# State-space decay: segment sums as two fp32r matmuls instead of one fp32 matmul

## The chip, the cores and the metric

The kernel runs on one core of a Trainium2 chip. The metric is the device time of one execution in microseconds, as the median of several runs of the same program. A program page and a trace of one profiled execution go with it; all rows below come from these.

## What is computed

The reference is a trunk of two layers on a sequence of 1024 tokens of width 1024. In each layer a normed input is projected, the columns go to four groups of heads (two kinds of attention, a state-space group and a gated delta group), their outputs are joined and projected back, and a feed-forward part with a convolution follows. The change lies in the state-space group, which runs once forward and once backward over the sequence in 8 chunks of 128 tokens, with 4 heads. The core of it, cut:

```
acum = cumsum(dt * A within a chunk)
seg = acum[..., :, None] - acum[..., None, :]        # segment sums
decay = exp(where(causal, seg, -inf))
scores = einsum('bcihn,bcjhn->bchij', Cc, Bc) * decay
y_diag = einsum('bchij,bcjhp->bcihp', scores, xc)
```

The rest of the scan (states at the chunk ends, their carry from chunk to chunk, `y_off`) is not touched.

## The kernel before

All tensors are fp32. A product that needs fp32 accuracy is mostly written as several matmuls over fp32r operands: the helper `splits` (L130) writes the high part of a tensor with ScalarE (L133, a copy into fp32r) and the low part with VectorE or GpSimd (L135, source minus high part). Some smaller products, the segment sums among them, are matmuls on plain fp32 operands.

A layer has a mixing part and a feed-forward part. In the mixing part `mix` (L1359) weaves nine streams of work by a table of start and end times, `when` (L439 on): `T` (transposed projections, L254 to L263), `nats` (other projections, `nat_step`, matmul L523, evacuated at L557 to L563), `d_prep` and `d_inverse` (set-up of the delta group, L848 to L931), `mixer_c` (the state-space group), `prep_a`, `att` (all attention: scores L1068, row maximum on VectorE L1070, exponential on ScalarE L1076, transposes L493 with their splits L133 and L135, product L1101), `mixer_d` and `prep_b`. The table gives the order in which the program is traced; after that a list scheduler with its own timing model orders the instructions of each engine, with the priorities that the tracing gave, and buffers are handed out from pools in that order. Each engine then runs its own list strictly in order (TensorE loads weights ahead), and waits on semaphores. So any change of a cost or of a pool's size can reorder the whole mixing part.

SBUF scratch comes from three pools by size, `slots = 34, 12, 24` (L55): 34 tiles of 4 KB per partition (`s4`), 12 of 2 KB (`s2`) and 24 of 1 KB (`s1`). The `s2` pool holds, among others, the split weights `wh` and `wl` of `load_T`, the buffers of `prep_a`, the query tiles of the attention, and the decay tiles `R`.

The state-space group has two halves. The first (L752 on) carries the states over the chunks. The second, the decay stage, goes chunk by chunk in three functions: `early(c + 1)` loads the next chunk and has GpSimd (POOL) write, per direction `d`, the tile `R` of 128 x 512: mask times gate (L780), then `X` (L737) and the skip term `xs` (L784). `decay(c)` makes the scores (matmul L792, masked by VectorE into `sm`, L796), the segment sums as one fp32 matmul of `R` with a triangular mask (L800, one per direction, 512 columns), their exponential on ScalarE back into `R` (L801), the product with `sm` on VectorE (L803), and the part from the carried state (matmul L806, VectorE L809, POOL L811 and L812 into `y`). `finish(c)` multiplies the decayed scores with `X` (L820), adds on VectorE (L821, L822), norms with POOL's power (L143, L144) and stores. Eight chunks in two directions give 16 matmuls of L800 per layer, 32 in the program.

The gates themselves (`ag`, 128 x 8 x 16) are made once per layer in `gates` (L689), from which `ex` and others are derived.

## Time and profile before

| what | value |
|---|---|
| median of 3 runs | 3188.63 us (3188.3 to 3191.51) |
| the profiled execution: span from first to last instruction | 3194.5 us |
| PE, weight loads, DVE, ACT, POOL busy | 95%, 80%, 61%, 39%, 25% |
| decay stage, layer 0 | 400.2 to 485.0 us |
| decay stage, layer 1 | 1987.6 to 2072.4 us |

No time of its own is recorded for the profiled execution beside its span; the span is 5.9 us above the median of the runs. To read it: busy shares are means over stages with different limits, so the rows by stage say more than the totals. PE's busy time counts a matmul to its modelled end, which overlaps with the next one; the time that a stream of matmuls really takes is the distance from start to start. The program places each layer's mixing part ahead of its feed-forward part: in layer 0 the mixing lasts to some 760 us, in layer 1 from 1600 to 2347 us.

### The profile page before, as it was taken

How to read it: one execution, taken by the hardware profiler on the slowest of the kernel's cores; microseconds unless marked ns; L12 is line 12 of the kernel's file. 1: busy time of each engine (PE TensorE's matmuls, PEld its weight loads, DVE VectorE, ACT ScalarE, POOL GpSimd, SP SyncE). 2: the span in 40 equal slices, each digit the busy share in tenths (PEclk: the TensorE clock that was granted, in tenths of full speed). 3: DMA queues.
4: the chain of work that ended last, by engine and by line, in shares of the span. 5: the costliest groups of instructions: out<-in, count | busy, mean ns of one | idle time of the engine just before them, and what ended most of it. 6: DMA issues, size and time to landing. Idle time of an engine off the chain costs nothing. (4 is left out here: it accounts for less than half of the span.)

```text
span 3194.5 us, 48801 instructions
## 1 busy us (share of the span) xinstructions
PE 3043.8 (95%) x18198; PEld 2550.7 (80%) x18198; DVE 1938.1 (61%) x3624; ACT 1251.9 (39%) x2615; POOL 789.4 (25%) x1253
## 2 busy tenths in 40 slices
PE   6998998999999999999999889999999999999997
PEld 6778777887888888888787777788878888888886
DVE  4556687686545555555565475876855455555556
ACT  3333355675432222222243333567743422222221
POOL 1266766221200000000143575753211000000003
PEclk9999999999999999999999998999999999999999
DMA  4255523232321111112232555232323112111212
GB/s 138 64 148 152 142 77 83 69 105 88 112 73 40 47 60 53 40 40 63 75 125 76 148 129 141 81 86 74 100 85 122 53 47 60 53 40 40 61 39 112
DMA packets 384561, 266.76 MB, mean 84 GB/s; under 512 B 147745, under 2 KB 353221, under 8 KB 384325
## 3 DMA queue, kind: packets, MB, share of 16 engines
q1 hardware_dynamic: 384324, 263.64, 28.5%
q8 instruction: 144, 2.36, 0.3%
q14 instruction: 93, 0.75, 0.1%
HBM read 194.54 MB, written 68.94 MB: 82 GB/s over the span
## 5 line engine op out<-in xcount | busy, mean ns | idle before, releaser
L263 PE MATMUL p<-hT,wh 128*128 128x512 f32 x3456 | 960.1, 392 | 7.1 <-ACT cy L388 2.6
L263 PEld LDWEIGHTS p<-hT,wh 128*128 128x128 f32 x3456 | 649.6, 189 | 144.8 <-ACT cy L388 3.4
L263 PE MATMUL p<-hT,wl 128*128 128x512 f32 x1728 | 553.2, 391 | 0.0
L263 PEld LDWEIGHTS p<-hT,wl 128*128 128x128 f32 x1728 | 325.2, 188 | 68.4 <-DVE wl L135 0.9
L221 POOL TENSOR_TENSOR acc<-acc,gain 128x768 f32<-128x768 f32 x14 | 28.9, 2066 | 1413.8 <-ACT junk L177 1413.8
L388 ACT ACTIVATE cy<-p,cw 128x1024 f32<-128x1024 f32 x88 | 106.0, 1204 | 589.7 <-PE p L263 589.7
L389 DVE SCALAR_TENSOR_TENSOR cy<-p,cw,cy 128x1023 f32<-128x1023 f32 x88 | 112.8, 1282 | 358.9 <-ACT cy L388 358.6
L523 PE MATMUL p<-wn,hT 128*128 128x256 f32 (+1 forms) x1920 | 291.1, 306 | 40.5 <-DVE pb L563 17.9
L523 PEld LDWEIGHTS p<-wn,hT 128*128 128x128 f32 x1920 | 266.6, 198 | 51.0 <-DVE pb L563 19.5
L135 DVE TENSOR_TENSOR pT<-pt,pT 128x512 fp32r<-128x512 f32 x256 | 172.6, 682 | 58.4 <-ACT pT L133 57.9
L133 ACT ACTIVATE wh<-raw 128x512 fp32r<-128x512 f32 x216 | 128.0, 624 | 187.1 <-PE p L263 93.3
L133 ACT ACTIVATE pT<-pt 128x512 fp32r<-128x512 f32 x256 | 150.6, 597 | 105.1 <-PE pt L493 95.1
L1070 DVE TENSOR_REDUCE nm<-p 128x1 f32<-128x1024 f32 x128 | 155.0, 1216 | 21.8 <-PE p L1068 21.6
L362 DVE TENSOR_TENSOR acc<-acc,p 128x512 f32<-128x512 f32 x160 | 109.3, 685 | 94.3 <-PE p L358 94.2
L362 DVE TENSOR_TENSOR acc<-acc,pt 128x512 f32<-128x512 f32 x160 | 109.5, 684 | 91.3 <-PE pt L358 89.3
L493 PE MATMUL pt<-ident,p 128*128 128x128 f32 x1024 | 154.5, 278 | 8.3 <-ACT p L1076 4.0
L1403 PE MATMUL p<-wo,oh 128*128 128x512 f32 x512 | 161.7, 394 | 0.3 <-ACT oh L133 0.3
L135 DVE TENSOR_TENSOR wl<-raw,wh 128x512 fp32r<-128x512 f32 x180 | 116.8, 685 | 64.7 <-ACT wh L133 64.7
L1076 ACT ACTIVATE p<-p,nm 128x1024 f32<-128x1024 f32 x128 | 142.3, 1112 | 15.0 <-DVE nm L1070 14.9
L493 PEld LDWEIGHTS pt<-ident,p 128*128 128x128 f32 x1024 | 117.4, 142 | 31.5 <-DVE pT L135 6.7
L358 PE MATMUL p<-owh,gh 128*128 128x512 f32 x352 | 138.6, 394 | 2.4 <-DVE acc L362 2.4
L358 PE MATMUL pt<-owh,gh 128*128 128x512 f32 x352 | 137.7, 391 | 2.9 <-DVE acc L362 2.8
(316 smaller groups left out, 5724.9 us busy)
## 6 DMA issues: line engine op xcount, KB each, us to landing
raw<-in_f_w_in_dram SPq DMA_DIRECT2D x176, 256.0 KB, 3.3
raw<-in_f_w_out_dram SPq DMA_DIRECT2D x88, 256.0 KB, 2.8
raw<-in_w_in_dram SPq DMA_DIRECT2D x72, 256.0 KB, 2.9
raw<-in_w_out_dram SPq DMA_DIRECT2D x32, 256.0 KB, 3.3
xr<-x_mid SPq DMA_DIRECT2D x16, 512.0 KB, 6.6
x_mid<-xr SPq DMA_DIRECT2D x14, 512.0 KB, 2.9
orow<-o_d SPq DMA_DIRECT2D x48, 128.0 KB, 3.0
pa<-pa_d SPq DMA_DIRECT2D x32, 176.0 KB, 3.6
```

Of the source, the lines that this page charges most:

```text
L133: nc.scalar.activation(out=hi, in_=src, func=AF.Copy)
L135: (eng or nc.vector).tensor_tensor(lo, src, hi.bitcast(F32), op=ALU.subtract)
L263: nc.tensor.matmul(pm[:, h * 512:(h + 1) * 512], s[:, k % 4, :], self.h_mov(p, k, h), start=a, stop=b)
L358: nc.tensor.matmul(po, s[i // 2][:, tk], w[:, cs], start=a, stop=b)
L362: nc.vector.tensor_tensor(acc[i][:, cs], acc[i][:, cs], po, op=ALU.add)
L388: nc.scalar.activation(out=y, in_=p, func=AF.Identity, scale=w1, bias=b)
L389: nc.vector.scalar_tensor_tensor(y[:, 1:], p[:, :n - 1], w0, y[:, 1:], op0=ALU.mult, op1=ALU.add)
L493: self.nc.tensor.transpose(pt[:n, t, :], src(4 * c + t), self.ident)
L523: self.nc.tensor.matmul(po, self.h_sta(a, k, i), wt[k][b], start=(k == 0 and a == 0 and b == 0), stop=(k == 7 and a == 1))
L1070: v.reduce_max(nm, s, axis=AX.X, negate=True)
L1076: nc.scalar.activation(out=p, in_=s, func=AF.Exp, bias=nm, accum_out=rs)
L1403: nc.tensor.matmul(y[:, cs], s[k // 2][:, k % 2, :], W[k][w][:, cs], start=(k == 0 and s is oh and w == 0), stop=(k == 7 and s is ol))
```

## The change

The gates of the state-space group are split once per layer into an fp32r high part and the fp32r remainder (`agc`, one ScalarE copy and one VectorE subtraction in `gates`). In `early`, POOL writes two tiles per direction, mask times high part and mask times low part (`Rp`, fp32r, 128 x 512 each), where it wrote one `R`. In `decay`, two fp32r matmuls accumulate into the same PSUM tile with the mask in fp32r (`maskR`, one ScalarE copy at the program's start). The exponential goes to a tile of the old `R` ring, no longer onto its own input. The two new rings take four more `s2` tiles, so that pool grows from 12 to 16; to make room the build reserves less SBUF for a DMA scratch that the SP queue's transfers go without. Three comment lines become empty.

```
-    slots = 34, 12, 24
+    slots = 34, 16, 24
...
+        self.maskR = self.t(self.cst, [128, 2, 128], F32R, "maskR")
+        nc.scalar.activation(out=self.maskR.rearrange("p d c -> p (d c)"), in_=m[:, 256:512], func=AF.Copy)
...
+        self.agc = self.par([128, 2, 8, 8], "agc")
+        nc.scalar.activation(out=self.agc[:, 0].bitcast(F32R), in_=ag[:, :, 0:8], func=AF.Copy)
+        v.tensor_tensor(self.agc[:, 1].bitcast(F32R), ag[:, :, 0:8], self.agc[:, 0], op=ALU.subtract)
...
+        rRh, rRl = (ring(lambda: self.s2([128, 4, 128], F32R, "Rp"), n) for n in (2, 2))
...
-                R = rR()
-                g.tensor_tensor(R, bc(self.mask[d], 1, 4), bc(self.ag[:, c, 4 * d:4 * d + 4], 2, 128), op=ALU.mult)
+                R = []
+                for k, r in ((0, rRh), (1, rRl)):
+                    R.append(r())
+                    g.tensor_tensor(R[k], bc(self.mask[d], 1, 4), bc(self.agc[:, k, c, 4 * d:4 * d + 4], 2, 128), op=ALU.mult)
...
-                nc.tensor.matmul(pseg, self.mask[2 + d], Rs[d], start=True, stop=True)
+                for k in range(2):
+                    nc.tensor.matmul(pseg, self.maskR[:, d], Rs[d][k], start=(k == 0), stop=(k == 1))
+                Rs[d] = rR()
                 nc.scalar.activation(out=Rs[d], in_=pseg, func=AF.Exp)
...
-    nc = _bacc.Bacc("TRN2", target_bir_lowering=False, num_devices=1)
+    nc = _bacc.Bacc("TRN2", target_bir_lowering=False, num_devices=1, dynamic_dma_scratch_size=1024)
```

The built order changes in both layers' mixing parts; in the feed-forward parts the transfers keep their order and some matmuls move by a few places. Line numbers of the changed kernel lie some 2 to 10 above those of the kernel before (its segment matmul is L809, its `Rp` L788).

On POOL in the decay stage of layer 0, one chunk, before: `R` per direction, with `X` (L737) between, then skip term, norm and the sum `y`.

```order
L780 TENSOR_TENSOR R_4051<-masks_292,ag_695 128x512
L737 TENSOR_TENSOR X_3368<-xs_3358,dt_693 128x256
L780 TENSOR_TENSOR R_4053<-masks_292,ag_695 128x512
L737 TENSOR_TENSOR X_3376<-xs_3358,dt_693 128x256
L143 TENSOR_SCALAR rs_588_4237<-ss_4234 128x1
L784 TENSOR_TENSOR xs_3358<-xs_3358,dsk_273 128x256
L144 TENSOR_TENSOR rs_588_4237<-rs_588_4237,mhalf_71 128x1
L811 TENSOR_TENSOR y_4045<-R_4042 128x256
L812 TENSOR_TENSOR y_4045<-y_4045,xs_3354 128x256
```

The same place after, on POOL:

```order
L145 TENSOR_SCALAR rs_594_4256<-ss_4253 128x1
L788 TENSOR_TENSOR Rp_3990<-masks_292,agc_699 128x512
L788 TENSOR_TENSOR Rp_3992<-masks_292,agc_699 128x512
L146 TENSOR_TENSOR rs_594_4256<-rs_594_4256,mhalf_71 128x1
L788 TENSOR_TENSOR Rp_3994<-masks_292,agc_699 128x512
L788 TENSOR_TENSOR Rp_3996<-masks_292,agc_699 128x512
L821 TENSOR_TENSOR y_4058<-R_4055 128x256
L822 TENSOR_TENSOR y_4058<-y_4058,xs_3359 128x256
L743 TENSOR_TENSOR X_3581<-xs_3367,dt_695 128x256
```

Four mask products stand ahead of the sum `y` (L811 before, L821 after) instead of two, the two `X` go behind it, and two of the products stand between the two halves of the norm (L143 and L144 before, L145 and L146 after).

On PE in the same stage, a later chunk, before: scores (L792), segment matmuls (L800), with a transpose of the attention (L493) between, and the matmul on the carried state (L806).

```order
L1320 MATMUL pt_4363<-ident_66,qn_3958 96x128 x4
L493 MATMUL pt_4379<-ident_66,p_4019 128x128 x4
L792 MATMUL p_589_4243<-cz_3364,bt_3360 128x256
L800 MATMUL p_590_4247<-R_3985,masks_292 128x512
L493 MATMUL pt_4386<-ident_66,p_4019 128x128 x4
L800 MATMUL p_591_4251<-R_3987,masks_292 128x512
L806 MATMUL p_592_4255<-Sin_3348,cz_3364 128x256 x2
```

After, on PE:

```order
L1330 MATMUL pt_4390<-ident_66,qn_3963 96x128 x4
L800 MATMUL p_595_4262<-cz_3369,bt_3365 128x256
L495 MATMUL pt_4406<-ident_66,p_4028 128x128 x4
L809 MATMUL p_596_4266<-Rp_3990,maskR_294 128x512
L809 MATMUL p_596_4266<-Rp_3992,maskR_294 128x512
L809 MATMUL p_597_4271<-Rp_3994,maskR_294 128x512
L809 MATMUL p_597_4271<-Rp_3996,maskR_294 128x512
L495 MATMUL pt_4413<-ident_66,p_4028 128x128 x4
L816 MATMUL p_598_4276<-Sin_3353,cz_3369 128x256 x2
```

Four matmuls in a row (two per direction) take the place of two with a transpose between; the scores (L792 before, L800 after) move one transpose forward.

On POOL ahead of the decay stage, some 136 us into layer 0, before: the scaled queries `th` (L629) of both directions, on which transposes on PE wait, and then the mask products of `d_prep` (L852).

```order
L135 TENSOR_TENSOR wl_1460<-raw_1457,wh_1459 128x512
L629 TENSOR_TENSOR th_985<-nat_988,ex_706 128x1024 x2
L852 TENSOR_TENSOR R_1535<-masks_292,ag_695 128x256 x2
L852 TENSOR_TENSOR R_1582<-masks_292,ag_695 128x256 x2
L135 TENSOR_TENSOR wl_1883<-raw_1880,wh_1882 128x512
```

After, on POOL:

```order
L137 TENSOR_TENSOR wl_1465<-raw_1462,wh_1464 128x512
L862 TENSOR_TENSOR R_1540<-masks_292,ag_697 128x256 x2
L862 TENSOR_TENSOR R_1587<-masks_292,ag_697 128x256 x2
L137 TENSOR_TENSOR wl_1888<-raw_1885,wh_1887 128x512
L631 TENSOR_TENSOR th_990<-nat_993,ex_711 128x1024
L866 TENSOR_TENSOR R_1540<-R_1540,masks_292 128x256 x2
L867 TENSOR_TENSOR R_1540<-R_1540,bt_670 128x256
L631 TENSOR_TENSOR th_990<-nat_993,ex_711 128x1024
```

`d_prep` has moved ahead of the queries, and three of its steps (L866 twice, L867) stand between the two directions' `th`.

## Rows read from the trace of the kernel before

**Rows 1.** page: span, busy time per engine, and the span in 40 slices

```profile
span 3194.5 us, 48801 instructions
PE 3043.8 (95%) x18198; PEld 2550.7 (80%) x18198; DVE 1938.1 (61%) x3624; ACT 1251.9 (39%) x2615; POOL 789.4 (25%) x1253
...
PE   6998998999999999999999889999999999999997
...
POOL 1266766221200000000143575753211000000003
PEclk9999999999999999999999998999999999999999
```

**Rows 2.** windows by stage: window, length, busy us (instructions) per engine, TensorE clock, DMA

```profile
0.00:400.00 400.00, 347.07 (x2399) 298.05 (x2400) 223.88 (x526) 147.59 (x311) 194.96 (x291) 0.94 0.47 128
400.20:485.00 84.80, 80.42 (x479) 63.31 (x479) 72.98 (x141) 46.77 (x107) 58.68 (x98) 0.98 0.29 79
485.00:760.00 275.00, 260.21 (x2468) 224.55 (x2467) 211.32 (x491) 188.43 (x424) 91.70 (x177) 0.99 0.31 84
760.00:1600.00 840.00, 828.05 (x3728) 684.15 (x3727) 449.09 (x658) 246.18 (x482) 36.28 (x56) 1.00 0.21 63
...
1987.60:2072.40 84.80, 80.44 (x478) 63.19 (x478) 72.99 (x141) 46.77 (x107) 58.67 (x98) 0.98 0.29 79
```

**Rows 3.** instructions of line 800, who waited: min/median/max ns

```profile
L800 PE MATMUL p<-R,masks x64: 590/593/1193, 400.5 to 2071.7; 128*128 128x512 f32 x64
...
  DVE sm L796: 3.9, 2
...
  ACT R L801: 19.6, 20
```

**Rows 4.** timeline, first chunk of the decay stage: start, us, engine, line

```profile
400.47 1.02 PE L800 MATMUL p<-R,masks 128*128 128x512 f32 x2
...
401.53 0.60 ACT L801 ACTIVATE R<-p 128x512 f32<-128x512 f32 x1 [0.94 <-PE p L800]
```

**Rows 5.** window in the feed-forward stage, fp32r matmuls of 512 columns only

```profile
1000.00:1200.00 200.00, 200.00 (x884) 165.62 (x883) 109.91 (x155) 51.25 (x89) 0.00 (x0) 1.00 0.16 48
```

**Rows 6.** groups by line in 400 to 485 us: busy, mean ns, idle before

```profile
L780 POOL TENSOR_TENSOR R<-masks,ag 128x512 f32<-128x512 f32 x13 | 14.0, 1074 | 4.2 <-PE p L820 3.2 <-ACT p L1076 1.1
L803 DVE TENSOR_TENSOR R<-R,sm 128x512 f32<-128x512 f32 x14 | 10.8, 774 | 0.4 <-ACT R L801 0.4
L811 POOL TENSOR_TENSOR y<-R 128x256 f32<-128x256 f32 x7 | 5.5, 785 | 19.2 <-DVE R L809 19.2
```

**Rows 7.** groups by line in 0 to 400 us: POOL writing fp32r tiles of 512

```profile
L135 POOL TENSOR_TENSOR wl<-raw,wh 128x512 fp32r<-128x512 f32 x18 | 23.9, 1335 | 39.6 <-ACT wh L133 38.0 <-DMA pa_d<-pa 1.5
```

**Rows 8.** waits in 400 to 485 us: total us, times, longest; DVE, then POOL

```profile
DVE rs L1077 <- ACT p L1076: 3.3, 3, 2.2
DVE y L821 <- PE p L820: 1.7, 2, 1.3
...
POOL y L811 <- DVE R L809: 19.2, 5, 6.5
POOL R L780 <- PE p L820: 3.2, 4, 1.2
```

**Rows 9.** two DVE lines with two SBUF inputs: min/median/max ns

```profile
L803 DVE TENSOR_TENSOR R<-R,sm x32: 667/688/1104, 402.2 to 2073.6; 128x512 f32<-128x512 f32 x32
L822 DVE TENSOR_TENSOR y<-y,zc x7: 411/681/1236, 410.1 to 483.2; 128x256 f32<-128x256 f32 x7
```

**Rows 10.** waits of PE in 0 to 400 us

```profile
PE p L523 <- DVE pb L563: 8.8, 4, 3.4
PE pt L493 <- POOL th L629: 4.8, 3, 2.1
```

**Rows 11.** groups by line in 0 to 400 us

```profile
L857 POOL TENSOR_TENSOR R<-R,bt 128x256 f32<-128x256 f32 x16 | 11.6, 740 | 0.0
L856 POOL TENSOR_TENSOR R<-R,masks 128x256 f32<-128x256 f32 x16 | 11.4, 734 | 9.4 <-ACT R L854 9.4
L629 POOL TENSOR_TENSOR th<-nat,ex 128x1024 f32<-128x1024 f32 x4 | 7.6, 1912 | 4.8 <-DVE nat L616 2.7 <-PE pt L493 2.0
```

## The prediction

> **What bounds the kernel now.** I read the page first. PE is busy for 95% of the span and in every slice but the first at least at eight tenths, at full clock nearly throughout; no other engine passes 61% [rows 1]. So a microsecond taken off PE's stream is worth up to a microsecond, if nothing else steps in where it is taken. Then the stages. The segment sums lie in the decay stage, 84.8 us in each layer, and the two layers give the same row but for hundredths [rows 2]. There PE is busy 80.4 us, but DVE has 73.0 (86%) and POOL 58.7 (69%), against 61% and 25% over the span: the change gives PE time back in a stretch in which two other engines are far fuller than elsewhere, and puts the work on one of them. After the stage PE has attention to do until 760 us with DVE at 211 of 275 us and POOL at a third, and then the feed-forward part, where only PE counts. Time won in the decay stage therefore stays won, unless it is lost before the attention takes over.
>
> **What the change takes off PE.** Each of the 32 fp32 matmuls of line 800 stands in the trace as two records of 593 ns [rows 3]. Two of them span 1.02 us, so the second starts 1.02 - 0.593 = 0.427 us after the first [rows 4]: that is the time that each record keeps the stream. An fp32r matmul of the same 512 columns takes 200 us / 884 = 0.226 us from start to start, with its weight load of 128 columns hidden, in a stretch where PE does nothing else [rows 5]. The change puts two fp32r matmuls where two records were, so 64 x (0.427 - 0.226) = 12.9 us leave PE, 6.4 us in each decay stage. The number of weight loads is the same. The chain to the exponential gets shorter too: ScalarE waits 19.6 us in 20 waits on these matmuls [rows 3], and from the start of the first record to the result it will be 0.226 + 0.39 where it was 1.02, some 0.4 us less. That helps those who wait and is not added to the sum.
>
> **What it adds on POOL.** 32 more mask products. One takes 1.07 us, and 13 of a layer's 16 lie in the stage [rows 6], the others just ahead of it. So POOL's 58.7 us become 58.7 + 14.0 = 72.7 us in a stage that should shrink to 84.8 - 6.4 = 78.4 us: 93%. The cover is there: POOL stands 19.2 us in this stage at line 811, waiting for VectorE's line 809, and 3.2 us for line 820 at the old `R` buffers [rows 8]. The order puts the four products of the next chunk right in front of that wait (the POOL rows of the section on the change), so they fill idle time, and the new rings are freed by the segment matmul itself and not by line 820. If that cover were gone, the 14.0 us would be paid in each layer. No row shows POOL writing fp32r from a mask and a broadcast; its fp32r subtraction of 512 columns, with two full inputs, takes 1.34 us [rows 7]. By that end the stage's 26 products cost 34.7 us where 13 now cost 14.0, and POOL needs 79.4 us, a little more than the shortened stage has. I take the 1.07 us, since shape and inputs are the same and only the type of the output differs, and keep the other for the range.
>
> **What it does to VectorE.** Nothing is added in the stage, but VectorE has only 84.8 - 73.0 = 11.8 us left there. It would have 78.4 - 73.0 = 5.4 us left if PE got its whole gain. And it gets slower where POOL works beside it. Line 803, which reads two SBUF tiles, takes 688 ns in the median and up to 1104; line 822 between 411 and 1236 [rows 9]; the mean of line 803 in the stage is 774 [rows 6]. With POOL at 93% instead of 69% I add 0.09 us (774 - 688, the delay that it has now, once more) on each of some 14 calls, and as much over the other lines of this kind together: 2 us or a bit more per stage, as an estimate; at the worst each of 14 calls waits 1104 - 688 = 0.42 us, 5.8 us. VectorE then needs 75 us of 78.4. Its waits come from chains that pass through PE and ScalarE (lines 1077, 821) [rows 8], of which some always remain. So I don't take the whole 6.4 us but two thirds, 4.2 us per layer: the stage then lasts 80.6 us with VectorE at 93%.
>
> The trace shows line 822 stretched to three times its shortest time while POOL runs [rows 9]. The Trainium skill (SBUF — State Buffer, Who interferes with whom) says that a VectorE instruction with two SBUF inputs and a GpSimd instruction that reads SBUF hold each other off for a whole instruction, by who starts first. That speaks against this change: by the mean of the rows the price is the 2 us above, by this rule at its hardest the one that the second rival works out below.
>
> **The rest.** `maskR` is one ScalarE copy of 256 columns before the first projections end; `agc` is one small copy and one small subtraction per layer, at 90 us, where PE has the projections to do. Both at nothing; without that cover under 1 us in all. The smaller DMA scratch: I count nothing, since every transfer that the page of the kernel before lists in this program's issues comes from SP's queue.
>
> **The order in front of the stage.** Four more 2 KB tiles let weights be split and loaded earlier, and the scheduler has reordered the first 400 us of each layer. PE idles 400 - 347 = 53 us there in layer 0 [rows 2], so something can be won or lost. Won: at the second pair of query tiles sixteen small matmuls now cover a wait. Lost: at the first pair (POOL's last rows in the section on the change) two calls of line 856 and one of 857, some 0.74 us each [rows 11], now stand ahead of the second `th`, so that a wait which takes part in the 4.8 us of [rows 10] can grow by up to 2.2 us, while the first one is covered better. The waits for evacuation (8.8 us in four waits, the longest 3.4) [rows 10] keep their causes. I take zero for the whole term, and for the range 3 us to either side per layer, about one such wait.
>
> **The sum.** Two layers at 4.2 us are 8.4 us. Against the profiled execution: 3194.5 - 8.4 = 3186.1 us of span. The median of the runs lies 5.9 us below that span; nothing in the change touches what makes that difference, so I carry it over: 3188.6 - 8.4 = 3180.2, **3180 us**, 0.27% faster. A measurement of this kernel can tell about 0.2%, 6.4 us, from no change.
>
> **The rivals.**
> 1. *POOL becomes the bound of the decay stage (slower).* The order of POOL is fixed, and the wait at line 811 can only be filled by products whose turn comes just there. Of POOL's idle time in the stage (84.8 - 58.7 = 26.1 us) the part that is not filled stays: with x us filled the stage lasts 72.7 + 26.1 - x. From x below 14.0 on it is longer than now. If a third of the 19.2 us fills, x = 6.4, the stage lasts 92.4 us and the kernel gets 2 x 7.6 = 15 us slower: 3204 us; with half, x = 9.6, 4.4 us per layer, 3197 us. For it: the sums `y` and the norm's power come later by up to two or four products, and lines 821 and 825 hold VectorE's whole queue when they are late. Against it: the products stand right at the long waits, and POOL runs a chunk ahead.
> 2. *VectorE eats the gain (no change).* If each of the 32 added products holds off one VectorE instruction by 0.42 us [rows 9], that is 13.4 us, and 12.9 us are won. That gives 3189 us; with half of it 3182. The same end comes if the chunks simply go at VectorE's pace. For it: VectorE is at 86% in the stage. Against: the median of line 803 is near its minimum now, with POOL at 69% [rows 9].
> 3. *All of it arrives, and the order gains too (faster still).* 12.9 us, and one of the waits ahead of the stage goes in each layer, 2 x 2 us: 3188.6 - 16.9 = 3172 us. For it: PE's idle ahead of the stage, and shorter chains to the exponential.
> 4. *The order loses in front of the stage what the stage wins (no change).* Two evacuation waits more of the longest kind, 2 x 3.4 us, against 8.4 us: 3187 us.
> 5. *The fp32r products don't run at 0.226 us here.* Only the shape of the moving tile differs from the rows that I took; I leave it 2 in 100, at no gain.
>
> **How the numbers follow.** Forecast (6.4 to 13 us won) 0.46; third rival 0.09; second and fourth together 0.29, with the fifth 0.31; first 0.14. Faster by over 0.2% is then 0.55, within 0.2% 0.31, slower 0.14. The range reaches from 3170 (the third rival and a little more) to 3196 us (the first rival with half of the wait filled), and leaves out about 0.2, mostly above.
>
> **What would show it.** In the changed profile the segment matmuls must be 64 records of about 390 ns. The decay stage (first to last segment matmul, 84 us now) should take near 80 us, with POOL over 90% and its wait at the sum `y` below 10 us instead of 19. If that wait stays and POOL's products are late, PE or VectorE will show waits named for POOL's `Rp` or `y`: the first rival. If line 803's mean goes to 0.9 us and above and VectorE passes 97%, it is the second. If the stage is shorter but its start comes later than 400 us, it is the fourth. The prediction is wrong in its main step if PE's wait at the segment matmuls, 3.9 us now for VectorE [rows 3], turns into one for POOL.

## The result, and the profile after

The changed kernel takes 3221.77 us (median of 4 runs, 3217.18 to 3223.95) beside 3188.95 us (four runs) for the kernel before, measured with it: ratio 1.0105, 95% interval 1.0090 to 1.0119. It is about 1%, 33 us, **slower**; forecast were 3180 us, at most 3196.

The profiled execution has a span of 3215.4 us, 20.9 us above that of before [rows 1]. This shows less than the medians do, because the profiled execution of before is longer than its timed runs and that of after is the shortest of its four. The groups in question in the decay stage of the kernel after (busy us, mean ns of one | idle before):

```profile
L788 POOL TENSOR_TENSOR Rp<-masks,agc 128x512 fp32r<-128x512 f32 x29 | 32.7, 1147 | 6.2 <-PE p L809 6.2
...
L813 DVE TENSOR_TENSOR R<-R,sm 128x512 f32<-128x512 f32 x16 | 19.7, 1240 | 0.7 <-ACT R L811 0.7
...
L809 PE MATMUL p<-Rp,maskR 128*128 128x512 f32 x32 | 12.3, 480 | 2.8 <-DVE sm L804 2.1 <-ACT R L811 0.8
```

POOL's waits there (us in total, times, longest):

```profile
POOL Rp L788 <- PE p L809: 6.2, 5, 2.5
...
POOL y L821 <- DVE R L819: 1.9, 2, 1.3
```

Busy time of PE, PEld, DVE, ACT and POOL by 20 us, then the granted clock:

```profile
360.00:380.00 20.00, 10.92 (x70) 9.00 (x69) 6.29 (x11) 5.52 (x10) 9.99 (x16) 0.89 0.45 122
380.00:400.00 20.00, 17.96 (x324) 13.58 (x324) 12.42 (x36) 5.54 (x13) 10.04 (x13) 0.69 0.53 143
400.00:420.00 20.00, 18.75 (x118) 15.90 (x115) 18.15 (x33) 14.01 (x27) 14.34 (x19) 1.00 0.21 58
420.00:440.00 20.00, 17.60 (x116) 15.35 (x116) 19.60 (x43) 11.44 (x26) 16.11 (x20) 0.92 0.31 91
440.00:460.00 20.00, 20.00 (x127) 17.16 (x126) 17.93 (x32) 10.75 (x22) 17.98 (x28) 0.99 0.27 75
460.00:480.00 20.00, 16.66 (x96) 14.19 (x95) 14.88 (x24) 10.17 (x29) 18.78 (x31) 0.91 0.25 67
480.00:500.00 20.00, 11.36 (x50) 7.63 (x48) 14.28 (x29) 3.80 (x10) 14.74 (x25) 0.62 0.22 58
```

The last two of these in the kernel before:

```profile
460.00:480.00 20.00, 18.82 (x127) 15.17 (x125) 14.77 (x26) 10.93 (x33) 16.55 (x33) 1.00 0.31 79
480.00:500.00 20.00, 15.64 (x132) 12.58 (x132) 17.35 (x45) 8.19 (x22) 16.82 (x33) 0.91 0.34 86
```

What the change was to do to TensorE, it does: the 64 records of the segment matmul have a median of 399 ns where there were 64 of 593 ns [rows 3], though 480 ns on the mean here, for the clock falls to 0.62 in 480 to 500 us. POOL's wait at the sum `y` is gone (1.9 us; it was 19.2 [rows 6]). And VectorE's product with `sm` takes 1240 ns on the mean in this stage, against 774 [rows 6].

The trace gives the start of every matmul, so the execution can be cut at matmuls that both kernels have. Two stretches per layer matter: **B**, from the first matmul of `Xi` in `d_inverse` (L930 before, L940 after) to the first segment matmul, and **C**, the decay stage, from there to the start of the last product of scores with `X` (L820 before, L830 after). In us, with the ratio of all timed runs:

| kernel | ratio | B, layer 0 | C, layer 0 | B, layer 1 | C, layer 1 |
|---|---|---|---|---|---|
| before | 1 | 48.8 | 91.6 | 49.0 | 93.0 |
| after | 1.0105 | 54.3 | 106.0 | 52.9 | 96.9 |

The rest of each layer differs by -4.3 to +0.6 us a part. So of 20.9 us the two decay stages lose 14.4 and 3.9 and the two stretches B ahead of them 5.5 and 3.9; the parts ahead of B win 2.3 and 4.3.

**Where the stage loses.** VectorE in the kernel after around 480 us (start, length):

```profile
478.77 2.62 DVE L813 TENSOR_TENSOR R<-R,sm 128x512 f32<-128x512 f32 x1
...
482.46 2.77 DVE L813 TENSOR_TENSOR R<-R,sm 128x512 f32<-128x512 f32 x1
485.15 0.74 DVE L819 TENSOR_TENSOR R<-p,ex 128x256 f32<-128x256 f32 x2
```

POOL at the same time:

```profile
478.67 0.61 POOL L984 TENSOR_TENSOR KM<-ident,ged 64x256 f32<-64x256 f32 x1
479.25 1.03 POOL L788 TENSOR_TENSOR Rp<-masks,agc 128x512 fp32r<-128x512 f32 x1
480.24 0.61 POOL L984 TENSOR_TENSOR KM<-ident,ged 64x256 f32<-64x256 f32 x1
480.81 2.48 POOL L788 TENSOR_TENSOR Rp<-masks,agc 128x512 fp32r<-128x512 f32 x2
483.26 2.70 POOL L137 TENSOR_TENSOR Vb<-raw,Vb 128x64 fp32r<-128x64 f32 x8
...
486.88 0.72 POOL L821 TENSOR_TENSOR y<-R 128x256 f32<-128x256 f32 x1
```

And TensorE, twice the same sixteen matmuls of two chunks (in brackets the wait before, and for whom):

```profile
471.09 1.90 PE L830 MATMUL p<-X,R 128*128 128x64 f32 x16
...
485.95 3.68 PE L830 MATMUL p<-X,R 128*128 128x64 f32 x16 [2.97 <-DVE R L819]
```

Two products of VectorE, 0.67 us long when nothing disturbs them, take 2.62 and 2.77 us, while POOL goes from instruction to instruction without a gap: `Rp`, a tile `KM` of the delta group, two more `Rp`, eight subtractions of `Vb`. Three POOL instructions pass before the first product gets through. The carried part (L819) stands behind them on VectorE, and TensorE waits 2.97 us for it. Then the sixteen matmuls of L830 take 3.68 us; the same sixteen had taken 1.90 us at 471 us. The granted clock of 480 to 500 us is 0.62 on the mean, so most of this stretch runs at the lower of its two levels, 1.2 GHz: in steps of 5 us it is 0.97 from 480 to 485 us, where TensorE is busy for 2.3 of the 5 us, and 0.50 in each step from there to 505 us. TensorE is busy for 13.2 of those last 20 us; at the ratio of 3.68 to 1.90 us, some 6 of them, as an estimate, are the price of the lower clock, of the 14.4 us that the stage loses.

**Where B loses.** TensorE's wait for the transfer that brings `Xi` back from DRAM was 1.4 us; it is now

```profile
PE p L940 <- DMA Xi<-x_d: 8.6, 1, 8.6
```

In layer 0 two things make this. TensorE has no other work left 4.8 us earlier (from 371.5 instead of 376.3 us on): it starts B 2.3 us earlier, and 105 matmuls of the projections (`nats`, L523 before, L525 after) stand in B where 124 stood, the rest having been moved ahead. And `Xi` is there 2.4 us later (380.1 against 377.7 us); why is not shown.

### The profile page after: what moved, and what is told of

It is laid out like the page before. It is cut to its first block, busy times and chain, and to the rows that moved or that the text cites. A ratio compares the mean times of both kernels' runs of the same rounds, so it can differ in the third digit from the quotient of the medians.

```text
span 3215.4 us, 48766 instructions
## 1 busy us (share of the span) xinstructions
PE 3043.8 (95%) x18198; PEld 2561.0 (80%) x18198; DVE 1946.4 (61%) x3626; ACT 1252.7 (39%) x2618; POOL 828.8 (26%) x1285
## 5 line engine op out<-in xcount | busy, mean ns | idle before, releaser
L525 PE MATMUL p<-wn,hT 128*128 128x256 f32 (+1 forms) x1920 | 293.8, 308 | 30.8 <-DVE pb L565 12.4
L525 PEld LDWEIGHTS p<-wn,hT 128*128 128x128 f32 x1920 | 270.0, 201 | 40.8 <-DVE hT L137 14.6
L137 DVE TENSOR_TENSOR pT<-pt,pT 128x512 fp32r<-128x512 f32 x256 | 173.4, 683 | 60.7 <-ACT pT L135 59.9
L495 PEld LDWEIGHTS pt<-ident,p 128*128 128x128 f32 x1024 | 117.8, 142 | 36.2 <-DVE pT L137 12.9
L360 PE MATMUL p<-owl,gh 128*128 128x512 f32 x352 | 138.1, 392 | 0.0
```

The lines of the kernel that those rows point to most:

```text
L137: (eng or nc.vector).tensor_tensor(lo, src, hi.bitcast(F32), op=ALU.subtract)
L360: nc.tensor.matmul(po, s[i // 2][:, tk], w[:, cs], start=a, stop=b)
L495: self.nc.tensor.transpose(pt[:n, t, :], src(4 * c + t), self.ident)
L525: self.nc.tensor.matmul(po, self.h_sta(a, k, i), wt[k][b], start=(k == 0 and a == 0 and b == 0), stop=(k == 7 and a == 1))
```

## Experiments

There are four questions: does POOL's second product cost the time, do the sixteen tiles of 2 KB and their order cost it, what is TensorE's saving worth, and by what mechanism does POOL's product act? All kernels stand in this table; B and C as above, from each kernel's profiled execution.

| kernel | what differs | ratio (95%) | B0 | C0 | B1 | C1 |
|---|---|---|---|---|---|---|
| `slots16` | before, 16 slots | 1.0042 (1.0027 to 1.0056) | 55.6 | 96.8 | 52.9 | 96.8 |
| `pool_twice` | the same, unread second product | 1.0080 (1.0056 to 1.0103) | 55.2 | 103.6 | 55.6 | 101.2 |
| `own_twice` | before, unread second product | 0.9990 (0.9981 to 0.9998) | 48.6 | 91.7 | 48.4 | 92.1 |
| `twice_chain` | before, second product in the path | 1.0117 (1.0094 to 1.0139) | 48.1 | 108.2 | 58.9 | 108.2 |
| `chain_first` | the same, chunks 0 to 3 | 1.0040 (1.0026 to 1.0053) | 47.7 | 93.6 | 58.0 | 93.7 |
| `chain_last` | the same, chunks 4 to 7 | 1.0083 (1.0069 to 1.0097) | 47.6 | 104.6 | 56.0 | 105.4 |
| `r_act` | before, `R` from ScalarE | 1.0011 (0.9999 to 1.0022) | 47.4 | 94.0 | 49.0 | 93.0 |
| `one_product` | high part only, 16 slots | 1.0032 (1.0019 to 1.0045) | 55.5 | 94.0 | 57.0 | 93.8 |
| `one_12` | high part only, 12 slots | 1.0017 (1.0007 to 1.0026) | 49.7 | 91.4 | 57.5 | 92.6 |
| `one_12_fp32` | the same, fp32 matmul | 1.0007 (0.9999 to 1.0016) | 48.0 | 92.6 | 49.3 | 93.7 |
| `one_12_chain` | `one_12`, second product in the path | 1.0073 (1.0051 to 1.0096) | 48.5 | 102.2 | 53.2 | 102.2 |
| `own_zero` | both matmuls, one product | 1.0042 (1.0028 to 1.0055) | 48.4 | 95.1 | 55.6 | 92.6 |
| `own_two` | after, 12 slots and own tiles | 1.0091 (1.0079 to 1.0104) | 48.1 | 98.6 | 59.8 | 106.5 |
| `two_14` | after, 14 slots | 1.0109 (1.0094 to 1.0124) | 53.8 | 97.7 | 59.3 | 100.6 |
| `low_act` | after, low product on ScalarE | 1.0064 (1.0042 to 1.0086) | 55.6 | 100.5 | 59.4 | 96.7 |
| `low_act_14` | the same, 14 slots | 1.0047 (1.0028 to 1.0066) | 55.1 | 92.0 | 58.4 | 97.7 |
| `own_low_act` | the same, 12 slots and own tiles | 1.0034 (1.0023 to 1.0046) | 47.6 | 92.1 | 47.9 | 94.0 |
| `exp_psum` | after, exponential left in PSUM | 1.0152 (1.0130 to 1.0174) | 53.8 | 110.2 | 59.9 | 108.4 |

Each kernel is scheduled anew, so each has an order of its own: `slots16`, in which no work differs, shows that this alone can be worth 13 us. Differences of a few us between two of these kernels are not read as an effect below; differences in C of 10 us and more, which come back in both layers, are. B and C don't hold the whole of every difference: those of `own_low_act` are those of before to 1.2 us, and its 0.34% lies elsewhere, in its profiled execution 5.0 us ahead of B in layer 0.

### The slots alone, and the load of POOL alone (not as meant)

```
-    slots = 34, 12, 24                 # slots16
+    slots = 34, 16, 24
...
-                R = rR()               # pool_twice (16 slots), own_twice (12, tiles of their own)
-                g.tensor_tensor(R, ...)
+                R = rR()
+                for r in (rX2(), R):
+                    g.tensor_tensor(r, ...)
```

> The kernel before with the 16 slots of 2 KB and the smaller DMA scratch alone; the products and the fp32 segment matmul stay as they were. Theory A (POOL's extra products cost the time, in the decay stage): 3183 to 3196 us, since the early stage's gain of 5 us and the 7 to 8 us lost at the end of d_inverse roughly cancel. Theory B (the larger pool's new order costs the time): 3205 us or more, most of the 33 us.

> The kernel before with 16 slots, and POOL writes each product R twice, the second time into a tile that nobody reads; the fp32 segment matmul stays. Theory A: 3215 to 3240 us, at least the changed kernel's time, because POOL's load is the changed kernel's and PE saves nothing; products of L803's kind of 2 us and more near the stage's end. Theory B: within 6 us of the kernel with 16 slots alone.

> The kernel before, its 12 slots and its order on TensorE unchanged to the instruction, with POOL writing every product R twice, the second time into four tiles of their own that nobody reads. The load of POOL alone. Theory A (POOL's second product costs 11 to 13 us, as between the 16-slot kernels with one and two): 3197 to 3202 us. Theory D (it costs only together with a new order): 3185 to 3191 us.

`slots16` (which has the smaller DMA scratch too, as have `pool_twice` and `own_twice`) lost 13 us (0.42%), between the two expectations: the slots are not the whole and not nothing. In layer 1 its B and C, 52.9 and 96.8 us, are those of after, 52.9 and 96.9: there the changed kernel loses no more than the 16 slots alone give, and POOL's products and TensorE's saving leave nothing that shows. Of these stretches only C of layer 0 is longer in after than in `slots16`, 106.0 against 96.8. B in layer 0 grows by 6.8 us, with the same wait for `Xi` as after (8.5 us); kernels with 12 slots keep B there at 47.4 to 49.7 us, all with 14 or 16 have 53.8 to 55.6.

`own_twice` (3184.7 us) seemed to say that POOL's load costs nothing, and `pool_twice` (3213.0 us, 2 us short of theory A's range) that it costs 12 us beside `slots16`. Neither tells it: nobody reads the second tile, so these products waited for nothing and ran elsewhere. In `own_twice` sixteen of them stand at 84 to 104 us, where POOL of the kernel before is busy for 6.0 of 20 us; in `pool_twice` they came in a block, POOL was busy for 20.00 of 20 us from 400 on, and in layer 1 a product of VectorE took 5.12 us beside four of them and a skip term in a row:

```profile
2016.28 5.12 DVE L805 TENSOR_TENSOR R<-R,sm 128x512 f32<-128x512 f32 x1
```

### The second product in its place

```
                 g.tensor_tensor(R, bc(self.mask[d], 1, 4), ..., op=ALU.mult)
+                g.tensor_tensor(R, R, bc(self.mask[d], 1, 4), op=ALU.mult)   # twice_chain
...
+                if c < 4:     # chain_first; chain_last has c >= 4; the same product under it
```

> The kernel before with POOL multiplying each R a second time by the mask, in place (the mask is 0 or 1, so R stays what it was): POOL's load of the changed kernel, in the path of the segment matmul, with fp32 matmuls, 12 slots and nothing else changed. Theory P (POOL's second product in its place is the cost): 3200 to 3218 us, VectorE's products with sm at 0.9 us or more on the mean. Theory Q (the second matmul and its order is the cost): 3184 to 3194 us.

> The kernel with the high part alone in one fp32r matmul and 12 slots, with POOL multiplying each product a second time by the mask, in place (the low part is left out): POOL's load of the changed kernel with the least work on PE. Theory P: 3207 to 3225 us, no faster than the same in fp32 (twice_chain), because PE's saving becomes waits. Theory Q: 3189 to 3198 us.

> The kernel before with POOL's second, idle multiplication of R by the mask for chunks 0 to 3 alone: 8 products of 1.04 us, 8.3 us per layer, where POOL waits 14.2 us at the sum y (400 to 440 us). Theory E (the cover lies ahead of 440 us): 3184 to 3194 us, no change. Theory L (each product costs about 1 us wherever it stands, by holding up VectorE): half of the 35 us of both halves, 3200 to 3208 us.

> The kernel before with POOL's second, idle multiplication of R by the mask for chunks 4 to 7 alone: 8.3 us per layer, where POOL waits 6.2 us at y and is busy for 83% of the time (440 to 492 us). Theory E: 3205 to 3222 us, nearly the whole loss, with a granted clock of 0.75 or less at the end of the stage. Theory L: 3200 to 3208 us, as for the first four chunks.

The kernel before, with POOL's second product and nothing else, loses 1.17% (3222 us, above the range of theory P), as much as the changed kernel; both its stages grow by 15 to 17 us. That POOL's load in its place costs the stage this much is shown; two things keep it from being the changed kernel's own sum. The second product of these kernels reads a full tile and takes 1.28 us in `chain_first` and 1.30 in `chain_last` (medians), where the change's takes 1.04, so they put about a quarter more on POOL than the change does. And after loses 14.4 us in C of one layer alone. Where in the stage the load stands decides: with the last four chunks C is 13.0 and 12.4 us longer, with the first four 2.0 and 0.7. Two windows of `chain_first` (columns as above):

```profile
460.00:480.00 20.00, 19.54 (x122) 15.04 (x120) 17.67 (x30) 11.49 (x32) 15.96 (x28) 1.00 0.31 77
480.00:500.00 20.00, 14.20 (x112) 11.29 (x111) 15.62 (x43) 8.99 (x23) 16.83 (x31) 0.95 0.34 90
```

The same of `chain_last`:

```profile
460.00:480.00 20.00, 15.71 (x103) 12.21 (x101) 17.16 (x22) 10.79 (x32) 19.42 (x36) 1.00 0.23 57
480.00:500.00 20.00, 15.75 (x67) 10.79 (x68) 14.48 (x43) 3.64 (x12) 12.28 (x20) 0.51 0.29 79
```

`chain_last` (3209.9 us) came as theory E said. With the load in the first half POOL is busy for 15.96 us from 460 to 480 and the clock stays at 0.95 afterwards; with the load in the second half it is 19.42 us, and the clock is 0.51. `chain_first` still is 0.4% slower, beyond the expectation of theory E and short of theory L. Its profiled execution doesn't lose this in C: B of layer 1 is 9 us longer than before, again by the wait for `Xi` (8.6 us). `one_12_chain` (3208.7 us) lies in the range of theory P, but not by its reason: it was to be no faster than `twice_chain`, and it is 13.6 us faster. TensorE's saving of 10 us per stage goes with a C that is 6.0 us shorter in both layers, and C stays 10.8 and 9.6 us above that of `one_12`.

### TensorE's saving

```
-                for k in range(2):      # one_product, one_12 (12 slots, two tiles for E): high part only
-                    nc.tensor.matmul(pseg, self.maskR[:, d], Rs[d][k], start=(k == 0), stop=(k == 1))
+                nc.tensor.matmul(pseg, self.maskR[:, d], Rs[d][0], start=True, stop=True)
...
+                nc.tensor.matmul(pseg, self.mask[2 + d], Rs[d][0], start=True, stop=True)   # one_12_fp32
...
+                    nc.tensor.matmul(pseg, self.maskR[:, d], (Rs[d][0], zR)[k], ...)   # own_zero: both, zR of zeros
```

> The changed kernel with the high part alone: one product on POOL and one fp32r matmul; the low part of the gates is left out of the segment sums. POOL's load is that of the kernel before, PE saves 27 - 7 = 20 us of segment matmuls. Theory A: 3168 to 3183 us (two thirds of the saving arrive, 3189 - 13 = 3176). Theory B: 3200 us or more, since the order of the 16 slots stays.

> The kernel before with 12 slots as it was, the gates rounded to fp32r, one product on POOL and one fp32r segment matmul (two tiles for the products, two for the exponentials, smaller DMA scratch); the low part is left out. Theory A (what PE saves in the decay stage arrives by two thirds): 20 us saved, 3168 to 3178 us. Theory C (the stage ends by a chain over POOL and VectorE, and PE's saving turns into waits and a lower clock): 3180 to 3191 us, with PE's busy time in 400 to 485 us down by 8 to 10 us and the last L820 no more than 3 us earlier.

> The kernel with 12 slots and the high part alone, but with its segment matmul in fp32 again (the low part is left out, as there): PE has 20 us more work, the rest is alike. Theory A: 10 us or more slower than the fp32r form, 3202 to 3212 us. Theory C (PE's saving in this stage turns into waits and a lower clock): within 4 us of the fp32r form or faster, 3184 to 3196 us.

> The changed kernel with 12 shared slots and product tiles of their own, where the second fp32r matmul reads a tile of zeros that is written once per layer (the low part is left out): both matmuls on PE, one product on POOL. Theory P: 3189 to 3200 us, as the kernels with one product. Theory Q: 3209 to 3220 us, as with both products on POOL (3217.5 us).

Theory A fell in the first three. `one_product`, at 3198.2 us, is 15 us above the range of theory A and 2 below that of theory B; `one_12`, at 3192.4, is 1.4 us above theory C's range, and `one_12_fp32`, at 3191.0, inside it. Between `one_12_fp32` and `one_12` TensorE loses 10 us of work in each stage, and the stage gets 1.2 and 1.1 us shorter. The whole program gets no faster (1.0007 to 1.0017), but of that B of layer 1, 8.2 us longer by the wait for `Xi`, is a part, so it is C that says what the saving is worth. Three windows show where the 10 us go; first those of `one_12_fp32`:

```profile
420.00:440.00 20.00, 18.78 (x119) 15.06 (x119) 17.54 (x39) 11.14 (x25) 12.60 (x17) 1.00 0.34 99
...
460.00:480.00 20.00, 17.77 (x124) 14.59 (x122) 14.61 (x27) 10.58 (x31) 18.07 (x36) 1.00 0.32 84
480.00:500.00 20.00, 17.19 (x141) 13.56 (x141) 16.90 (x45) 8.13 (x23) 16.06 (x31) 0.91 0.31 80
```

The same of `one_12`:

```profile
420.00:440.00 20.00, 17.39 (x110) 14.68 (x109) 17.54 (x39) 10.84 (x25) 14.04 (x17) 0.91 0.31 90
...
460.00:480.00 20.00, 15.89 (x102) 12.56 (x101) 15.24 (x34) 10.18 (x30) 17.26 (x34) 0.86 0.32 84
480.00:500.00 20.00, 15.90 (x131) 14.07 (x130) 13.59 (x32) 7.56 (x23) 17.25 (x34) 0.80 0.30 82
```

TensorE with less to do waits more, the granted clock falls from 1.00 to 0.91 and 0.86 in two windows and from 0.91 to 0.80 in the third, and the other matmuls take longer. VectorE and POOL have the same work in both. `own_zero` (3200.6 us, 0.6 above the range of theory P), with both matmuls, still has C at 95.1 and 92.6 us; its 0.42% are mostly B of layer 1.

This is not the rule for every kernel here. With POOL's second product in the path the same saving came through in part: 13.6 us of 20 from `twice_chain` to `one_12_chain`, and 0.26%, 8 us, of 13 from `twice_chain` to `own_two`, whose second product is also the shorter one. These pairs differ in their order and in the instructions of VectorE that are held up (below), so what the saving alone is worth in a stage with POOL's double load stays open.

### The low products off POOL, and the slots apart

```
+                        for h in range(4):      # low_act, low_act_14, own_low_act, for k == 1
+                            nc.scalar.activation(out=R[k][:, h], in_=self.mask[d], func=AF.Copy, scale=self.agc[...])
...
-    slots = 34, 16, 24      # two_14, low_act_14 (with two tiles for E); own_two, own_low_act: 12
+    slots = 34, 14, 24
...
-            self.s2([128, 4, 128], F32R, "Rp")      # own_two, own_low_act
+            self.mem.tile([128, 4, 128], F32R, tag="own", ..., bufs=4)
```

> The changed kernel with 16 slots, the low part's products on ScalarE (four copies of 128 x 128 with a scale each, in the place of one product on POOL); POOL's load is that of the kernel before. Theory A (POOL's extra products cost 11 to 15 us): 3195 to 3208 us, no product of VectorE in the stage over 1.6 us. Theory B (the order that comes with two fp32r matmuls costs it, whoever writes the low tile): 3214 us or more.

> As the kernel with the low products on ScalarE, but 14 slots, with two tiles for the exponentials in place of four, so that as many slots are left to the other work as in the kernel before. Theory A: 3188 to 3200 us, below the 16-slot form, if the freed slots' order costs the 13 us that 16 slots alone cost. If two exponential tiles are too few, a wait of ScalarE or VectorE at the exponential appears and the time is 3205 us or more.

> The changed kernel with 14 slots and two tiles for the exponentials, both products on POOL. Theory A: POOL's part of the loss stays, the slots' part goes by some of its 13 us: 3205 to 3220 us. Theory B (only the order matters): anywhere from 3190 to 3235 us, with no product on VectorE longer than 1.6 us needed for a loss.

> The changed kernel, with the four product tiles in a place of their own, so that the 12 shared slots are again left to the other work as before. If the 13 us that 16 slots cost alone add to the rest, 3222 - 13 = 3205 to 3212 us; if the loss is POOL's and the order of the two matmuls' alone, 3215 to 3225 us. Against the kernel with the second product and fp32 in 12 slots: PE saves 13 us, theory A wants it 8 us or more faster, theory C (the saving becomes idle time and a lower clock) within 4 us or slower.

> The changed kernel with 12 shared slots, four product tiles of their own, and the low products on ScalarE, so that neither POOL's load nor the slots differ from the kernel before. If the losses add: 3222 - 13 - 12 = 3192 to 3200 us; if PE's saving of 13 us then arrives by two thirds, 3178 to 3184 us; if ScalarE's 128 copies cost more than POOL's product, 3200 us or more.

Few of these came as expected: `low_act` (3210.5 us) and `low_act_14` (3202.7) lie between their two ranges, `two_14` (3222.4) 2 us above that of theory A, `own_two` (3217.5) in the range without the slots' 13 us, and `own_low_act` (3200.1) at the border of two. Off POOL, the low product costs 0.57% less with 12 slots (`own_two` to `own_low_act`, 18 us) and 0.41% less with 16 (after to `low_act`, 13 us), although ScalarE needs 1.6 us for what POOL did in 1.04. The slots: `own_two` has B of layer 0 back at 48.1 us, yet is only 4 us faster than after, less than the 13 expected, and `two_14` none. `two_14` loses as much as after although no instruction of VectorE is stretched by more than 1 us in its stages, so a loss of this size also comes without the long holds of the next section. The losses do not add. The best form of the whole change, `own_low_act`, keeps 0.34%. None beats the kernel before; nor did the last of the side ways, POOL freed in the kernel before:

```
-                g.tensor_tensor(R, ...)      # r_act
+                for h in range(4):
+                    nc.scalar.activation(out=R[:, h], in_=self.mask[d], func=AF.Copy, scale=self.ag[...])
```

> The kernel before with R written by ScalarE (four copies of 128 x 128 with a scale, 0.40 us each) and not by POOL, fp32 matmul, 12 slots. If POOL's load limits the stage already in the kernel before: 3172 to 3184 us. If the stage has POOL to spare at one product per direction: 3185 to 3200 us, the longer writing of R (1.6 us against 1.04) being the only difference.

It is no faster (1.0011, in the second range): with one product per direction, freeing POOL wins nothing, at least not against ScalarE's slower writing of `R`.

### How POOL holds up VectorE

```
-                nc.scalar.activation(out=Rs[d], in_=pseg, func=AF.Exp)      # exp_psum
-                v.tensor_tensor(E, E, bc(sms[d], 2, 2), op=ALU.mult)
+                nc.scalar.activation(out=pseg, in_=pseg, func=AF.Exp)
+                v.tensor_tensor(Rs[d]..., pseg..., bc(sms[d], 2, 2), op=ALU.mult)
```

> The changed kernel, but the exponential stays in PSUM (written onto its own input) and VectorE's product with sm reads it from there, so that this product has one SBUF input and not two; POOL's work is unchanged. Theory A1 (POOL's back-to-back instructions hold off VectorE's instruction with two SBUF inputs): the 2.6 and 2.8 us products fall to 0.9 us or less each, the time falls to 3190 to 3207 us. Theory A2 (POOL's queue is simply too long, and y, X and the norm come late): the product gets shorter, but the time stays at 3214 to 3230 us. Theory B: also 3214 to 3230 us.

The product of this kernel (ns: shortest, median, longest):

```profile
L812 DVE TENSOR_TENSOR R<-p,sm x32: 665/674/692, 404.9 to 2115.3; 128x512 f32<-128x512 f32 x32
```

The same product of the changed kernel:

```profile
L813 DVE TENSOR_TENSOR R<-R,sm x32: 673/1046/2770, 405.2 to 2090.0; 128x512 f32<-128x512 f32 x32
```

With one input in PSUM and one in SBUF it is never held, with POOL's load unchanged. But the hold has moved to another instruction with two SBUF inputs, the norm's last step. VectorE in `exp_psum`:

```profile
481.47 4.40 DVE L834 SCALAR_TENSOR_TENSOR y<-y,rs,og 128x256 f32<-128x256 f32 x1
```

POOL beside it:

```profile
481.22 1.37 POOL L983 TENSOR_TENSOR KM<-ident,ged 64x256 f32<-64x256 f32 x2
482.55 3.03 POOL L788 TENSOR_TENSOR Rp<-masks,agc 128x512 fp32r<-128x512 f32 x3
485.55 1.60 POOL L137 TENSOR_TENSOR Vb<-raw,Vb 128x64 fp32r<-128x64 f32 x5
```

So the kernel got slower than after, not faster (3237.8 us, above all three ranges); it also keeps each PSUM tile until VectorE has read it, and what share that has was not separated. The first theory (A1) is right about the instruction and wrong about the time.

In `twice_chain` the same happens with fp32 matmuls. VectorE:

```profile
476.80 4.05 DVE L826 SCALAR_TENSOR_TENSOR y<-y,rs,og 128x256 f32<-128x256 f32 x1
```

POOL:

```profile
476.49 1.18 POOL L975 TENSOR_TENSOR KM<-ident,ged 64x256 f32<-64x256 f32 x2
477.63 1.26 POOL L781 TENSOR_TENSOR R<-R,masks 128x512 f32<-128x512 f32 x1
478.86 0.31 POOL L135 TENSOR_TENSOR Vb<-raw,Vb 128x64 fp32r<-128x64 f32 x1
479.13 0.60 POOL L785 TENSOR_TENSOR xs<-xs,dsk 128x256 f32<-128x256 f32 x1
479.70 2.33 POOL L135 TENSOR_TENSOR Vb<-raw,Vb 128x64 fp32r<-128x64 f32 x6
```

And TensorE in `chain_last`:

```profile
481.49 3.68 PE L822 MATMUL p<-X,R 128*128 128x64 f32 x16 [3.48 <-DVE R L811]
```

An instruction that takes 0.47 us at its shortest takes 4.05 us; in `chain_last` one of 4.06 us is followed by TensorE's wait of 3.48 us and by sixteen matmuls at the lower clock. Over all kernels the two things go together, with an overlap at the border: each stage in which one of these instructions of VectorE takes 2.5 us or more (after in layer 0, `own_two` in layer 1, both layers of `pool_twice`, `twice_chain`, `chain_last`, `exp_psum`) has C at 101.2 to 110.2 us; in every other stage C lies between 91.4 and 102.2. The closest pair is two layers of one kernel: after, 106.0 with the hold and 96.9 without; `own_two`, 106.5 with and 98.6 without. By these two pairs the hold would be worth some 8 to 9 us and the rest of POOL's load some 4 to 7 us per stage. `one_12_chain` does not fit that: its C is 10.8 and 9.6 us above that of `one_12` with no such hold, only with products of VectorE that take up to 1.8 us, POOL busy for 56.9 of the 60 us from 440 to 500, and a clock of 0.54 in the last 20 of them. No kernel took the hold away alone, so it is shown that the hold comes from POOL's load, and not what share of the loss it is.

## Why the prediction was wrong

**TensorE's saving (12.9 us, two thirds to arrive).** The size was right, 399 ns a record where 390 were forecast. The two thirds were a choice and not a reading, and what arrives was not fixed by the stage: from `one_12_fp32` to `one_12` a stage that saves 10 us gains 1.2, from `twice_chain` to `one_12_chain` 6.0. In the first pair the time taken off TensorE became waiting time, and the wait had a price of its own, since the granted clock fell with it (1.00 to 0.91 and 0.86). The prediction's sum has no term for the clock.

**POOL's products (13 of 1.07 us in 19.2 us of cover).** The price was right: 1.04 us, for the fp32r type no more, so the 1.34 us of the upper bound [rows 7] did not come. The step that failed is the sum of the cover over the whole stage. Read in halves, 400 to 440 us and 440 to 492 us of the kernel before, POOL's wait at `y` is

```profile
POOL y L811 <- DVE R L809: 14.2, 3, 6.5
...
POOL y L811 <- DVE R L809: 6.2, 3, 2.7
```

and of the second 1.3 us come after 485 us. In this half prep_b's and the delta group's work joins POOL's queue, and eight products of 1.04 us do not fit into the wait. `chain_first` and `chain_last` show it, with a product that is a quarter longer: 2.0 and 0.7 us in C against 13.0 and 12.4. In the changed kernel it came so in layer 0; in layer 1 C is no longer than that of `slots16`, and that the same load did less there is not explained.

**VectorE (2 us per stage).** Mis-sized: the 16 products with `sm` alone cost 19.7 - 12.1 = 7.6 us more in layer 0 (12.1 us are all 16 of before; [rows 6] has 14 of them), above the 5.8 us that stood there as the worst. The bound took the longest hold of line 803 in the kernel before, 0.42 us [rows 9], for the longest there can be, though line 822 beside it, 411 to 1236 ns, was already held for 0.83. Both were measured where POOL's queue had gaps; in the traces above a hold goes on over several of POOL's instructions where there are none.

**The order in front of the stage (zero, 3 us to either side).** On balance 3.2 us lost in layer 0, just outside the bounds, and 0.4 won in layer 1; it is made of a gain ahead of B and a larger loss in B. The prediction has no term for the transfer of `Xi`, for which TensorE waited only 1.4 us; part of what hid it were the matmuls that moved. The larger omission is that the term ended where the stage begins: `slots16`, with the same work, has C 5.2 and 3.8 us longer. The smaller DMA scratch costs nothing that shows (`own_twice` has it, at 0.9990); the gates and `maskR` no kernel separates.

**The rivals.** The first (POOL becomes the bound, priced at 3204 us) is the nearest to what came, with marks of the second and fourth: POOL's wait at `y` fell from 19.2 to 1.9 us, but that was its cover used up and not the sign of success it was named as. Line 813's mean passed 0.9 us as the second asked, though VectorE was busy for 85% of the stage and not 97%. The start of the stage came at 403.8 us. From the first to the last segment matmul the stage took 90.9 us in layer 0 and 84.2 in layer 1, where 80 were forecast. The sign for the main step, a wait of TensorE at the segment matmuls for VectorE that turns into one for POOL, was no clean one: in the kernel before, 5.4 us of the waits at L800 are named for POOL beside 3.9 for VectorE, and after, at L809, 8.1 beside 4.2. The price of the first was too low: it counts POOL's time that is not covered, and the hold of VectorE, the wait of TensorE and the lower clock behind it come on top. The second had the right mechanism with a bound too small, and treated it as something that could at most eat the gain.

What stays open: why the same loads, in other orders, differ by up to some 10 us. B of layer 1 is 47.9 to 49.3 us in five kernels, before among them, with a wait for `Xi` of 1.4 to 4.6 us, and 52.9 to 59.9 in all others, with one of 8.0 to 9.0. No kernel holds the projections in place with the changed work. Nor is it shown what `Xi` waits for.

## What to carry to other kernels

Read an engine's slack per chunk and not per stage: a wait that lies in the first half of a stage is no cover for work in its second half, and here eight more products in the last four chunks cost the stage 12 to 13 us where eight in the first four cost 1 to 2. A saving on TensorE need not arrive where other engines are nearly as full as it is. Test it with the matmul alone first (one product, one matmul): here that gave 1 us of 10 per stage and nothing in the program, before POOL got any more to do. Where every edit gives a new order, have one kernel that changes the order and no work: here it lost 13 us, and without it that loss would be put down to the work. And before adding instructions to POOL, look where its queue runs without a gap beside VectorE instructions with two SBUF inputs, because the price there can be several POOL instructions (VectorE instructions of 2.6 to 5.1 us here), not a part of one.

## What the runs showed of the hardware

VectorE instructions with two SBUF inputs, 0.41 to 0.67 us long at their shortest, took 2.6 to 5.1 us while three and more POOL instructions in a row went past; with one input in PSUM the product with `sm` took 665 to 692 ns in all 32 calls beside the same load. The Trainium skill (SBUF — State Buffer, Who interferes with whom) says that such an instruction contends with a POOL instruction that reads SBUF, and that one with a single SBUF input doesn't. The traces agree with both. The Trainium skill's wording that whichever of the two starts first has the ports for the whole instruction (SBUF — State Buffer, SBUF: two separate sides) lets one expect a hold of one POOL instruction, 1.04 us here; the 2.62, 4.05 and 5.12 us measured are longer, so the wait goes on over POOL's next instructions where these follow without a gap.

In one pair of kernels TensorE's extra work cost no time: the fp32 form of the segment matmul, 20 us more of TensorE's time over the program, ran in the same time as the fp32r form (`one_12_fp32` and `one_12`, 3191.0 and 3192.4 us), at a mean granted clock of 0.980 against 0.976 in their profiled executions.
